# A two-block transformer on one core: expert outputs scaled as they leave PSUM and scattered by a one-hot matrix in two float32r parts

## The chip, the core and the metric

The kernel runs on one core of a Trainium2 chip. The core has a matrix engine (TensorE, "PE" in the profile; its weight loads appear as "PEld"), a vector engine (VectorE, "DVE"), a scalar engine (ScalarE, "ACT"), GpSimd ("POOL") and SyncE ("SP"), which here issues the weight DMAs. They share an on-chip memory, SBUF; PE writes its products to PSUM, and the other engines read them there. An f32 product takes PE several passes; a product of two "float32r" operands takes one, and a sum of a high and a low float32r part keeps nearly the precision of f32. The metric is the device time of one execution in microseconds (us).

## The reference

Two blocks follow each other on 256 tokens of width 1024. The first is an mLSTM mixer and a mixture of experts (MoE), the second a mixer of two kinds of attention and a feed-forward net. The change is in the experts. Each of 32 experts serves the tokens that have it among their four best, and its output is added to the token, times a gate:

```python
gate = xb @ w_gate[e] + b_gate[e]
up = xb @ w_up[e] + b_up[e]
gate = jnp.minimum(gate, SWIGLU_LIMIT)
up = jnp.clip(up, -SWIGLU_LIMIT, SWIGLU_LIMIT)
glu = gate * jax.nn.sigmoid(SWIGLU_ALPHA * gate)
return (glu * (up + 1.0)) @ w_down[e] + b_down[e]
...
y_buf = y_buf * gate_buf[:, None].astype(y_buf.dtype)
out = jax.ops.segment_sum(y_buf, tok_buf, num_segments=T + 1)[:T]
```

The weights of the experts are 32 x 12 MB of f32, and every one is read from HBM once.

## The kernel before

The first mixer and the router run until about 124 us, the experts from there to 1060 us, the second block to the end at 1650 us.

**Weights.** All weights of the program come through one ring of slots of 1 MB, in the order of their use (class `Ring`). SP's queue issues a slot's DMA as soon as the slot that it reuses is free (`refill`, called behind the products that used it). An expert has twelve such loads: four for `w_gate`, four for `w_up`, four for `w_down`.

**Tokens.** An expert works on at most CAP = 64 tokens at once. Two experts form a pair. `group(g)` makes the one-hot matrix `oh` of a pair (which token stands at which of the 128 places), gathers the tokens by products with it into `xg`, 128 columns at a time, multiplies the one-hot matrix by the gates (`og`, L1031) and transposes that with four PE transposes (L1040) into `sc`. A small scheduler hands out the steps of the next pair's `group` between the products of the current experts: `start` adds a generator, and `tick`, called after each slot of an expert's `up`, runs its next steps. `later`, which the kernel has for other stages, adds a function in the same way.

**An expert.** `up(e)` takes eight slots: sixteen products into `ps_g`, sixteen into `ps_u` (one PSUM buffer each, pool `psg`). `down(e-1)` begins: four transposes of the hidden vector into `ps_t`, and DVE's copy `ht`. `hidden(e)` calls `swiglu`, five operations on DVE and ACT, which read `ps_g` and `ps_u` and keep their temporary, `sg`, in SBUF. Then the four slots of `down(e-1)` follow, sixteen products into `ps_y`, and ACT copies those to `y`. After the second expert of a pair `down` also scatters: four f32 products of `sc` with `y` into `ps_x` (128 x 512 each), and four additions on DVE into the activations `x` (L1110).

```python
for e in range(n):
    ...
    for _ in up(e):
        ...
    if e:
        d = down(e - 1)
        next(d)
    hidden(e)
    if e:
        for _ in d:
            pass
```

Expert 0 has no `down` before it: expert 1's `up` follows expert 0's directly on PE.

**The biases of `w_down`.** `b_down()` computes gates times biases for all experts at once: two transposes of the gates (L996), and four f32 products added to `x` (L1004). Its 128 KB are loaded ahead of the experts, and the scheduler hands its steps out during experts 0 and 1.

**The end of the experts.** After the last scatter PE runs filler products of `ones` (`warm`, 14 of them, two passes each), then comes `overflow()`. That is code for experts with over 64 tokens; a branch on the largest count (L1159) jumps over it, as it does for these inputs. Behind the branch's target PE runs 12 more fillers, into `ps_b`, and then the twelve transposes of `fv` (L1309) with which the second block begins. The lines L106 and L109 are the helpers `act` and `mm`, through which most ACT operations and products go.

Of the kernel before, what the change touches and what calls it, by code (L numbers as in the profile page):

```python
# [92 lines left out]
class Kernel:  # L93
# [77 lines left out]
    def consts(self):  # L171
# [7 lines left out]
                                fill=1.0, base=0, channel_multiplier=1)  # L179
        self.nhalf = c.tile([128, 1], F32, name="nhalf")  # L180
# [745 lines left out]
    def top_gates(self, ps):  # L926
# [13 lines left out]
        for tb in range(2):  # L940
            v.tensor_scalar(out=gate[:, tb, :], in0=gate[:, tb, :], scalar1=sm[:, tb:tb + 1], scalar2=None,
                            op0=OP.mult)
        self.first_slot = p.tile([128, 2], F32, name="first_slot")
# [34 lines left out]
    def experts(self):  # L978
        nc, tc, a, x = self.nc, self.tc, self.a, self.x
        v = nc.vector  # L980
        with ExitStack() as ctx:
# [5 lines left out]
            pst = self.pool("mot", bufs=1, space=PSUM, ctx=ctx, reuse_waits="tile")  # L987

            bd = q.tile([E, D], F32, tag="y", name="bd", bufs=1)
            nc.scalar.dma_start(out=bd, in_=a["b_down"][0])  # L990
            gt = q.tile([E, T], F32, tag="ht", name="gt", bufs=1)

            def b_down():
# [4 lines left out]
                yield 2  # L998
                for tb in range(2):
                    for dh in range(2):  # L1000
# [4 lines left out]
                        yield  # L1005

            GR = 2
            xg, sc = {}, {}

            def group(g):  # L1010
# [9 lines left out]
                s = sc[g] = q.tile([128, GR // 2, 2, T], F32, tag="sc", name="sc")  # L1020
# [8 lines left out]
                og = q.tile([128, 2, GR // 2, 3, CAP], F32, tag="og", name="og", bufs=1)  # L1029
                for tb in range(2):  # L1030
                    v.tensor_tensor(out=og[:, tb, :, 0:2, :], in0=oh[:, tb].rearrange("p (a b) s -> p a b s", b=2),  # L1031
                                    in1=self.gate[:, tb, e0:e0 + GR].rearrange("p (a b) -> p a b", b=2)[
                                        :, :, :, None].to_broadcast([128, GR // 2, 2, CAP]), op=OP.mult)
                    nc.gpsimd.tensor_copy(og[:, tb, :, 2, :], og[:, tb, :, 0, :])
                yield 2
                for pr in range(GR // 2):
                    ps = psx.tile([128, 2, T], F32, tag="x", name="ps_x")
                    for i in range(2):
                        for tb in range(2):
                            nc.tensor.transpose(ps[:, i, tb * 128:(tb + 1) * 128],  # L1040
# [34 lines left out]
            def down(e):  # L1075
# [9 lines left out]
                if not odd:  # L1085
                    ys[e // 2] = q.tile([128, 2, 512], F32, tag="y", name="y", bufs=1)
# [1019 lines left out]
```

## Time and profile before

| | |
|---|---|
| median of 3 runs | 1653.11 us (1653.06 to 1653.57) |
| the profiled execution | 1652.3 us |
| its span, from first to last instruction | 1650.6 us |
| its mean granted TensorE clock | 0.994 |
| PE busy, share of the span | 95% |
| DVE, ACT, POOL busy | 42%, 32%, 3% |
| HBM traffic | 505.74 MB read, 307 GB/s over the span |

The shares are means over stages with different limits: the experts move over 400 GB/s, the second block under 210. Windows and timelines of a stage tell more than the totals. In a timeline, a row has its start, its length, the engine, the line, the operation, its output and inputs, and in brackets the idle time ahead of it and what ended that. The granted clock is a share of full speed: 1.00 is 2.4 GHz, 0.50 is 1.2 GHz.

### The profile page before, as it was taken

How to read it: one execution, taken by the hardware profiler on the slowest of the kernel's cores; microseconds unless marked ns; L12 is line 12 of the kernel's file. 1: busy time of each engine (PE TensorE's matmuls, PEld its weight loads, DVE VectorE, ACT ScalarE, POOL GpSimd, SP SyncE). 2: the span in 40 equal slices, each digit the busy share in tenths (PEclk: the TensorE clock that was granted, in tenths of full speed). 3: DMA queues.
4: the chain of work that ended last, by engine and by line, in shares of the span. 5: the costliest groups of instructions: out<-in, count | busy, mean ns of one | idle time of the engine just before them, and what ended most of it. 6: DMA issues, size and time to landing. Idle time of an engine off the chain costs nothing. (4 is left out here: it accounts for less than half of the span.)

```text
span 1650.6 us, 22396 instructions
## 1 busy us (share of the span) xinstructions
PE 1567.6 (95%) x8810; PEld 950.9 (58%) x8811; DVE 695.4 (42%) x1437; ACT 524.9 (32%) x1151; POOL 54.8 (3%) x124
## 2 busy tenths in 40 slices
PE   8999999999999999999999998799999999999997
PEld 8783333333333333333323322489888999989996
DVE  6862212212121212122121121388875376777775
ACT  4562111111111111111111110256663356565554
POOL 0100000000000000000000010000111010000000
PEclk9999999999999999999999999999999999999999
DMA  8878999999999999999999999644343333556551
GB/s 285 305 307 310 408 418 421 421 422 421 420 422 420 421 421 422 421 420 421 421 421 421 421 421 421 271 131 155 124 153 103 103 120 137 179 166 202 182 187 69
DMA packets 119235, 508.31 MB, mean 308 GB/s; under 512 B 10364, under 2 KB 33717, under 8 KB 70101
## 3 DMA queue, kind: packets, MB, share of 16 engines
q1 hardware_dynamic: 117284, 506.01, 77.8%
q8 instruction: 71, 1.16, 0.3%
q10 hardware_dynamic: 1840, 0.82, 0.2%
q14 instruction: 40, 0.32, 0.1%
HBM read 505.74 MB, written 1.05 MB: 307 GB/s over the span
## 5 line engine op out<-in xcount | busy, mean ns | idle before, releaser
L349 DVE TENSOR_TENSOR lo<-w,hi 128x512 fp32r<-128x512 f32 (+2 forms) x380 | 257.3, 691 | 56.9 <-PE ps_d L109 30.6
L1081 DVE COPY ht<-ps_t 128x512 f32<-128x512 f32 x32 | 22.1, 692 | 596.5 <-PE ps_t L1079 596.5
L109 PE MATMUL ps_y<-w,ht 128*64 128x512 f32 x1024 | 230.1, 597 | 29.8 <-DVE ht L1081 25.1
L106 ACT ACTIVATE hi<-w 128x512 fp32r<-128x512 f32 (+2 forms) x380 | 232.1, 628 | 74.8 <-PE ps_d L109 67.2
L109 PE MATMUL ps_g<-w,xg 128*64 128x512 f32 x1024 | 238.3, 600 | 6.1 <-DMA w<-in_w_gate_dram 4.9
L109 PE MATMUL ps_u<-w,xg 128*64 128x512 f32 x1024 | 238.0, 600 | 2.9 <-DMA w<-in_w_up_dram 2.8
L109 PEld LDWEIGHTS ps_y<-w,ht 128*64 128x64 f32 x1024 | 69.2, 136 | 170.0 <-issue 113.6
L106 ACT ACTIVATE xg<-ps_x,n2p 128x128 f32<-128x128 f32 x128 | 47.0, 368 | 334.3 <-PE ps_x L109 334.0
L109 PEld LDWEIGHTS ps_g<-w,xg 128*64 128x64 f32 x1024 | 67.1, 136 | 135.2 <-issue 101.0
L109 PEld LDWEIGHTS ps_u<-w,xg 128*64 128x64 f32 x1024 | 66.1, 136 | 116.6 <-issue 96.3
L109 PEld LDWEIGHTS ps_x<-oh,xn 128*128 128x128 f32 x512 | 68.7, 190 | 78.2 <-issue 64.7
L106 ACT ACTIVATE y<-ps_y 64x512 f32<-64x512 f32 x64 | 37.9, 592 | 186.7 <-PE ps_y L109 186.1
L109 PE MATMUL ps_x<-oh,xn 128*128 128x128 f32 x512 | 86.9, 294 | 0.8 <-DVE oh L1016 0.8
L106 ACT ACTIVATE sg<-gg 128x512 f32<-128x512 f32 x32 | 20.1, 629 | 200.4 <-DVE gg L1262 200.3
L1110 DVE TENSOR_TENSOR x<-x,ps_x 128x512 f32<-128x512 f32 x64 | 43.9, 686 | 91.9 <-PE ps_x L109 91.9
L109 PE MATMUL ps_d<-hnh,hi 128*128 128x256 f32 x448 | 77.7, 295 | 0.8 <-ACT hi L106 0.5
L109 PE MATMUL ps_d<-hnh,lo 128*128 128x256 f32 x448 | 71.5, 281 | 3.2 <-DVE lo L349 3.1
L109 PE MATMUL ps_d<-hnl,hi 128*128 128x256 f32 x448 | 71.1, 281 | 0.0
L109 PE MATMUL ps_x<-y,sc 128*128 128x512 f32 x128 | 59.2, 605 | 11.1 <-ACT y L106 11.1
L109 PEld LDWEIGHTS ps_d<-hnh,hi 128*128 128x128 f32 x448 | 61.5, 189 | 3.5 <-ACT hi L106 0.6
L109 PEld LDWEIGHTS ps_d<-hnh,lo 128*128 128x128 f32 x448 | 60.7, 188 | 4.0 <-DVE lo L349 3.8
L109 PEld LDWEIGHTS ps_d<-hnl,hi 128*128 128x128 f32 x448 | 60.8, 188 | 0.2
(435 smaller groups left out, 2079.3 us busy)
## 6 DMA issues: line engine op xcount, KB each, us to landing
w<-in_w_down_dram SPq DMA_DIRECT2D x137, 1024.0 KB
w<-in_w_gate_dram SPq DMA_DIRECT2D x128, 1024.0 KB
w<-in_w_up_dram SPq DMA_DIRECT2D x128, 1024.0 KB
w<-in_w_in_dram SPq DMA_DIRECT2D x40, 1024.0 KB
w<-in_w_up_dram SPq DMA_DIRECT2D x44, 512.0 KB
w<-in_w_out_dram SPq DMA_DIRECT2D x8, 1024.0 KB
w<-in_w_branch_gdn_dram SPq DMA_DIRECT2D x4, 1024.0 KB
w<-in_w_branch_fox_dram SPq DMA_DIRECT2D x4, 1024.0 KB
```

The costliest lines, as they stand in the source:

```text
L106: self.nc.scalar.activation(out=out, in_=in_, func=func, **kw)
L109: self.nc.tensor.matmul(out, lhsT=lhsT, rhs=rhs, start=start, stop=stop, **kw)
L349: nc.vector.tensor_tensor(out=lo[:, :n], in0=src, in1=hi[:, :n].bitcast(F32), op=OP.subtract)
L1081: v.tensor_copy(ht, ps)
L1110: v.tensor_tensor(out=o, in0=o, in1=ps, op=OP.add)
```

## The change

The gate no longer goes into the matrix that scatters. `og` is now the one-hot matrix itself in bf16. A new generator `back(g)`, run in the second expert of a pair, transposes it by four bf16 products with an identity (`ident16`, one per program) into `sc`, and gets the gate of each place by four more small products, with the gates cut into three bf16 parts (`gate3`), which DVE sums to `gc`. As `ps_y` leaves PSUM, ACT multiplies it by the gate into `y`, a float32r tile, and DVE computes what that rounding lost into a second one, `yl`. The scatter is then two float32r products, with `y` and `yl`, where it was one f32 product. For all pairs but the third and the last it is handed to `later`, which spreads it over the next expert's `up`. `b_down` is loaded at the end of the loop's turn for expert 6 (counted from 0) and summed in the turn of expert 7, the eighth, between its `up` and the products of `down(6)`. Because the tiles' memory is needed elsewhere, `swiglu` gets its temporary from its caller: in the experts this is `ps_g` itself.

```diff
-
-            bd = q.tile([E, D], F32, tag="y", name="bd", bufs=1)
-            nc.scalar.dma_start(out=bd, in_=a["b_down"][0])
-            gt = q.tile([E, T], F32, tag="ht", name="gt", bufs=1)
-
             def b_down():
+
+                bd = q.tile([E, D], F32, tag="y", name="bd", bufs=1)
+                nc.scalar.dma_start(out=bd, in_=a["b_down"][0])
+                yield
+                gt = q.tile([E, T], F32, tag="ht", name="gt", bufs=1)
                 ps = psx.tile([128, 512], F32, tag="x", name="ps_x")
                 for tb in range(2):
                     nc.tensor.transpose(ps[0:E, tb * 128:(tb + 1) * 128], self.gate[:, tb, :], self.ident)
                 v.tensor_copy(gt, ps[0:E, 0:T])
-                yield 2
+                yield
                 for tb in range(2):
                     for dh in range(2):
                         ps = psx.tile([128, 512], F32, tag="x", name="ps_x")
                         self.mm(ps, gt[:, tb * 128:(tb + 1) * 128], bd[:, dh * 512:(dh + 1) * 512])
                         o = x[:, tb, dh * 512:(dh + 1) * 512]
                         v.tensor_tensor(out=o, in0=o, in1=ps, op=OP.add)
-                        yield
 
             GR = 2
-            xg, sc = {}, {}
+            xg, og, sc, gc = {}, {}, {}, {}
...
-                s = sc[g] = q.tile([128, GR // 2, 2, T], F32, tag="sc", name="sc")
...
-                og = q.tile([128, 2, GR // 2, 3, CAP], F32, tag="og", name="og", bufs=1)
-                for tb in range(2):
-                    v.tensor_tensor(out=og[:, tb, :, 0:2, :], in0=oh[:, tb].rearrange("p (a b) s -> p a b s", b=2),
-                                    in1=self.gate[:, tb, e0:e0 + GR].rearrange("p (a b) -> p a b", b=2)[
-                                        :, :, :, None].to_broadcast([128, GR // 2, 2, CAP]), op=OP.mult)
-                    nc.gpsimd.tensor_copy(og[:, tb, :, 2, :], og[:, tb, :, 0, :])
-                yield 2
-                for pr in range(GR // 2):
-                    ps = psx.tile([128, 2, T], F32, tag="x", name="ps_x")
-                    for i in range(2):
-                        for tb in range(2):
-                            nc.tensor.transpose(ps[:, i, tb * 128:(tb + 1) * 128],
-                                                og[:, tb, pr].rearrange("p e s -> p (e s)")[:, i * CAP:i * CAP + 128],
-                                                self.ident)
-                    self.act(s[:, pr], ps)
-                    yield
+                o = og[g] = q.tile([128, 2, 3, CAP], BF16, tag="og", name="og", bufs=1)
+                v.tensor_copy(o[:, :, 0:2, :], oh)
+                v.tensor_copy(o[:, :, 2, :], oh[:, :, 0, :])
+
+            def back(g):
+
+                o = og.pop(g).rearrange("p b e s -> p b (e s)")
+                s = sc[g] = q.tile([128, 2, T], F32R, tag="sc", name="sc", bufs=1)
+                c = gc[g] = q.tile([128, 2, 2], F32, tag="gc", name="gc", bufs=1)
+                ps = psx.tile([128, 2, T], F32, tag="x", name="ps_x")
+                for i in range(2):
+                    for tb in range(2):
+                        self.mm(ps[:, i, tb * 128:(tb + 1) * 128], o[:, tb, i * CAP:i * CAP + 128], self.ident16)
+                self.act(s, ps)
+                yield
+                ps = psx.tile([128, 512], F32, tag="x", name="ps_x")
+                for i in range(2):
+                    for tb in range(2):
+                        self.mm(ps[:, i * 6:i * 6 + 6], o[:, tb, i * CAP:i * CAP + 128],
+                                self.gate3[:, tb, g * GR:g * GR + GR, :].rearrange("p e k -> p (e k)"),
+                                start=tb == 0, stop=tb == 1)
+                v.tensor_reduce(out=c, in_=ps[:, 0:12].rearrange("p (i e k) -> p i e k", i=2, e=2),
+                                axis=mybir.AxisListType.X, op=OP.add)
...
             def hidden(e):
                 gg = q.tile([128, 512], F32, tag="gg", name="gg", bufs=1)
-                self.swiglu(gg, *hs[e])
+                self.swiglu(gg, *hs[e], hs[e][0])
                 hs[e] = gg
...
                 odd = e % 2
                 if not odd:
-                    ys[e // 2] = q.tile([128, 2, 512], F32, tag="y", name="y", bufs=1)
-                y = ys[e // 2]
+                    ys[e // 2] = [q.tile([128, 2, 512], F32R, tag=t, name=t, bufs=1) for t in ("y", "yl")]
+                y, yl = ys[e // 2]
+                c = gc[e // 2]
...
                 for h in range(2):
                     r = (h ^ odd) * 64
-                    self.act(y[r:r + 64, h, :], pa[r:r + 64, :])
+                    self.act(y[r:r + 64, h, :], pa[r:r + 64, :], scale=c[r:r + 64, h, odd:odd + 1])
+                for h in range(2):
+                    r = (h ^ odd) * 64
+                    v.scalar_tensor_tensor(out=yl[r:r + 64, h, :], in0=pa[r:r + 64, :], scalar=c[r:r + 64, h, odd:odd + 1],
+                                           in1=y[r:r + 64, h, :].bitcast(F32), op0=OP.mult, op1=OP.subtract)
                 if odd:
-                    yield
-                    g, i = divmod(e - 1, GR)
-                    for h in range(2):
-                        for tb in range(2):
-                            ps = psx.tile([128, 512], F32, tag="x", name="ps_x")
-                            self.mm(ps, sc[g][:, i // 2, h, tb * 128:(tb + 1) * 128], y[:, h, :])
-                            o = x[:, tb, h * 512:(h + 1) * 512]
-                            v.tensor_tensor(out=o, in0=o, in1=ps, op=OP.add)
-                            if e == n - 1:
-                                rest.append(self.mid_sums(xsq, gf2, h, tb))
-                                for gen in rest[-2:]:
-                                    next(gen, None)
+                    if e in (n - 1, B_DOWN - 1):
+                        for _ in scatter(e):
+                            yield
+                    else:
+                        self.later(1, scatter, e)
+
+            def scatter(e):
+                y, s = ys.pop(e // 2), sc[e // 2]
+                for h in range(2):
+                    for tb in range(2):
+                        ps = psx.tile([128, 512], F32, tag="x", name="ps_x")
+                        for i in range(2):
+                            self.mm(ps, s[:, h, tb * 128:(tb + 1) * 128], y[i][:, h, :], start=i == 0, stop=i == 1)
+                        o = x[:, tb, h * 512:(h + 1) * 512]
+                        v.tensor_tensor(out=o, in0=o, in1=ps, op=OP.add)
+                        if e == n - 1:
+                            rest.append(self.mid_sums(xsq, gf2, h, tb))
+                            for gen in rest[-2:]:
+                                next(gen, None)
                         yield
...
                 if e % GR == 0 and e + GR < n:
                     self.start(group(e // GR + 1))
-                for _ in up(e):
+                way = iter(back(e // GR)) if e % GR else None
+                bd = b_down() if e == B_DOWN else bd
+                for k, _ in enumerate(up(e)):
                     if e == 0 and first:
                         for _ in range(2):
                             if next(first, 0) == 0:
                                 first = None
-                                self.start(b_down())
                                 break
                     else:
                         self.tick(2 if e < 2 * GR else 1)
+
+                    if way and k > 4:
+                        next(way, None)
+                if bd and e > B_DOWN:
+                    for _ in bd:
+                        pass
+                    bd = None
                 if e:
                     d = down(e - 1)
                     next(d)
@@ -1139,6 +1174,8 @@
                 if e:
                     for _ in d:
                         pass
+                if e == B_DOWN:
+                    next(bd)
             self.drain()
...
-    def swiglu(self, gg, pg, pu, paired=False):
+    def swiglu(self, gg, pg, pu, t, paired=False):

 
         v = self.nc.vector
-        t = self.mow.tile([128, 512], F32, tag="sg", name="sg", bufs=1)
...
+B_DOWN = 6
```

PE at the end of expert 0 and the start of expert 1, before (`ps_g` and `ps_u` are the products of `up`, `oh` those of the gather, `lg` the gates, `bd` the biases):

```order
L1040 MATMUL ps_x<-ident,og 128x128 x4
L109 MATMUL ps_u<-w,xg 64x512 x8
L996 MATMUL ps_x<-ident,lg 32x128 x2
L109 MATMUL ps_u<-w,xg 64x512 x4
L109 MATMUL ps_x<-oh,xn_1557 128x128 x2
L109 MATMUL ps_u<-w,xg 64x512 x4
L109 MATMUL ps_u<-bias,pick 128x512
L109 MATMUL ps_x<-bd,gt 128x512
L109 MATMUL ps_x<-oh,xn_1557 128x128 x2
L109 MATMUL ps_g<-w,xg 64x512 x4
```

The same place with the change:

```order
L109 MATMUL ps_u<-w,xg 64x512 x8
L109 MATMUL ps_x<-oh,xn_1559 128x128 x2
L109 MATMUL ps_u<-w,xg 64x512 x4
L109 MATMUL ps_x<-oh,xn_1559 128x128 x2
L109 MATMUL ps_u<-w,xg 64x512 x4
L109 MATMUL ps_u<-bias,pick 128x512
L109 MATMUL ps_x<-oh,xn_1559 128x128 x2
L109 MATMUL ps_g<-w,xg 64x512 x4
```

The transposes of `og` and of the gates and the bias product are gone from here, and one more step of the gather stands ahead of expert 1.

DVE from one expert's `ht` over `swiglu` on, before:

```order
L1081 COPY ht<-ps_t 128x512
L1262 TENSOR_SCALAR gg<-ps_g 128x2x128x2
L1264 TENSOR_TENSOR gg<-gg,sg 128x512
L1268 TENSOR_SCALAR sg<-ps_u 128x2x128x2
L1269 SCALAR_TENSOR_TENSOR gg<-sg,gg 128x512
```

And with the change:

```order
L1095 COPY ht<-ps_t 128x512
L1298 TENSOR_SCALAR gg<-ps_g 128x2x128x2
L1300 TENSOR_TENSOR gg<-gg,ps_g 128x512
L1304 TENSOR_SCALAR ps_g<-ps_u 128x2x128x2
L1305 SCALAR_TENSOR_TENSOR gg<-ps_g,gg 128x512
L1119 SCALAR_TENSOR_TENSOR yl<-ps_y,gc,y 64x512 x2
```

The last reader of `ps_g` is now the fourth of the DVE operations, not the first, and two operations for `yl` follow.

PE at the end of the experts, before (the last `down`, the scatter, the fillers, the branch of L1159):

```order
L109 MATMUL ps_y<-w,ht 64x512 x16
L109 MATMUL ps_x<-y,sc 128x512 x4
L109 MATMUL ps_x<-ones 128x128 x14
L1158 TENSOR_LOAD cmax
L1159 COMPARE_AND_BRANCH
```

With the change:

```order
L109 MATMUL ps_y<-w,ht 64x512 x16
L109 MATMUL ps_x<-y,sc 128x512
L109 MATMUL ps_x<-yl,sc 128x512
L109 MATMUL ps_x<-y,sc 128x512
L109 MATMUL ps_x<-yl,sc 128x512
L109 MATMUL ps_x<-y,sc 128x512
L109 MATMUL ps_x<-yl,sc 128x512
L109 MATMUL ps_x<-y,sc 128x512
L109 MATMUL ps_x<-yl,sc 128x512
L109 MATMUL ps_x<-ones 128x128 x14
L1195 TENSOR_LOAD cmax
L1196 COMPARE_AND_BRANCH
```

The scatter's four products are now eight; the fillers and the branch follow as before.

## Rows read from the trace of the kernel before

**Rows 1.** Windows: stretch, us, PE, PEld, DVE, ACT, POOL busy, clock, DMA share, GB/s.
```profile
949.00:990.00 41.00, 37.25 (x160) 12.16 (x158) 9.24 (x14) 4.47 (x9) 5.09 (x4) 1.00 1.01 422
1072.00:1114.00 42.00, 41.52 (x304) 36.97 (x303) 34.45 (x81) 25.10 (x52) 4.00 (x8) 1.00 0.41 128
```

**Rows 2.** The page: GB/s in 40 equal slices of the span.
```profile
GB/s 285 305 307 310 408 418 421 421 422 421 420 422 420 421 421 422 421 420 421 421 421 421 421 421 421 271 131 155 124 153 103 103 120 137 179 166 202 182 187 69
```

**Rows 3.** Waits of PE, 900 to 1000 us: us in all, how many, the longest.
```profile
PE ps_g L109 <- DMA w<-in_w_gate_dram: 3.3, 6, 0.6
```

**Rows 4.** Timeline of PE: the transposes of og, and a scatter.
```profile
561.38 0.60 PE L1040 MATMUL ps_x<-ident,og 128*128 128x128 f32 x4
...
606.32 3.70 PE L109 MATMUL ps_x<-y,sc 128*128 128x512 f32 x8 [0.69 <-ACT y L106]
```

**Rows 5.** Timeline of PE: float32r products of the first mixer.
```profile
100.33 0.40 PE L109 MATMUL ps_o<-hi,yph 128*128 128x512 f32 x1
100.56 0.40 PE L109 MATMUL ps_o<-lo,yph 128*128 128x512 f32 x1
```

**Rows 6.** Timeline: one down on PE, the last operation of swiglu on DVE.
```profile
570.65 7.09 PE L109 MATMUL ps_y<-w,ht 128*64 128x512 f32 x32 [0.78 <-DVE ht L1081]
...
574.15 0.69 DVE L1269 SCALAR_TENSOR_TENSOR gg<-sg,gg 128x512 f32<-128x512 f32 x1
```

**Rows 7.** Windows of 5 us at the start of the stream.
```profile
125.00:130.00 5.00, 4.99 (x31) 2.54 (x31) 1.69 (x12) 2.09 (x7) 0.41 (x2) 1.00 0.36 115
...
180.00:185.00 5.00, 5.00 (x26) 1.91 (x24) 0.00 (x0) 2.28 (x5) 0.00 (x0) 1.00 0.99 403
```

**Rows 8.** Timeline: the end of expert 0 and the start of expert 1.
```profile
146.24 1.12 PE L109 MATMUL ps_x<-bd,gt 32*128 32x512 f32 x2
...
148.00 1.03 DVE L1262 TENSOR_SCALAR gg<-ps_g 128x512 f32<-128x512 f32 x1
...
148.43 1.28 ACT L106 ACT_TABLE_LOAD   x1
...
149.09 1.94 PE L109 MATMUL ps_g<-w,xg 128*64 128x512 f32 x8 [1.09 <-DVE gg L1262]
...
149.72 0.63 ACT L106 ACTIVATE sg<-gg 128x512 f32<-128x512 f32 x1
```

**Rows 9.** Timeline: the last scatter on ACT and DVE.
```profile
1053.32 1.21 ACT L106 ACTIVATE y<-ps_y 64x512 f32<-64x512 f32 x2 [8.13 <-PE ps_y L109]
...
1055.13 0.69 DVE L1110 TENSOR_TENSOR x<-x,ps_x 128x512 f32<-128x512 f32 x1 [9.92 <-PE ps_x L109]
```

**Rows 10.** Timeline: the handover from the experts to the second block.
```profile
1057.50 3.29 PE L109 MATMUL ps_x<-ones 128*128 128x128 f32 x28
...
1061.24 1.24 PE L109 MATMUL ps_b<-ones 128*128 128x128 f32 x9 [0.45 <-PEq L1159]
...
1064.49 0.34 DVE L1302 TENSOR_SCALAR fv<-x,nr 128x256 f32<-128x256 f32 x1
...
1066.41 3.57 PE L109 MATMUL ps_b<-ones 128*128 128x128 f32 x15 [3.93 <-issue]
...
1069.77 2.44 PE L1309 MATMUL ps_t<-ident,fv 128*128 128x128 f32 x12
```

**Rows 11.** DMA queues, 1062.5 to 1066.4 us: packets, MB, share of 16 engines.
```profile
q8 instruction: 1, 0.02, 1.9%
```

**Rows 12.** Windows: the rest of the fillers and the transposes.
```profile
1066.40:1072.00 5.60, 5.59 (x28) 5.60 (x28) 0.26 (x1) 1.14 (x3) 0.00 (x0) 0.52 0.02 5
```

**Rows 13.** The page: busy us and instructions by engine; the queue of instructions.
```profile
PE 1567.6 (95%) x8810; PEld 950.9 (58%) x8811; DVE 695.4 (42%) x1437; ACT 524.9 (32%) x1151; POOL 54.8 (3%) x124
...
q8 instruction: 71, 1.16, 0.3%
```

**Rows 14.** Timeline of PE: the first twelve transposes of the program.
```profile
9.85 1.59 PE L1309 MATMUL ps_t<-ident,qk 128*128 128x128 f32 x12 [0.65 <-DVE qk L1298]
```

**Rows 15.** A window of 5 us late in the experts.
```profile
1010.00:1015.00 5.00, 3.53 (x17) 0.91 (x14) 0.00 (x0) 0.86 (x2) 0.00 (x0) 1.00 1.01 419
```

More of the change, by code (lines that the diff above doesn't have):

```diff
@@ L179, in consts @@
                                 fill=1.0, base=0, channel_multiplier=1)
+        self.ident16 = c.tile([128, 128], BF16, name="ident16")
+        nc.vector.tensor_copy(self.ident16, self.ident)
         self.nhalf = c.tile([128, 1], F32, name="nhalf")
@@ L942, in top_gates @@
                             op0=OP.mult)
+        self.gate3 = p.tile([128, 2, E, 3], BF16, name="gate3")
+        rest = p.tile([128, 2, E], F32, name="grest", tag="gate")
+        v.tensor_copy(self.gate3[:, :, :, 0], gate)
+        v.tensor_tensor(out=rest, in0=gate, in1=self.gate3[:, :, :, 0], op=OP.subtract)
+        v.tensor_copy(self.gate3[:, :, :, 1], rest)
+        v.tensor_tensor(out=self.gate3[:, :, :, 2], in0=rest, in1=self.gate3[:, :, :, 1], op=OP.subtract)
         self.first_slot = p.tile([128, 2], F32, name="first_slot")
@@ L1064, in up @@
                         if k0 == KD - 2:
-                            self.mm(ps, pick.rearrange("p h s -> p (h s)"), self.bias[:, m, :], start=False, stop=True,
-                                    skip_group_check=True)
+                            self.mm(ps, pick.rearrange("p h s -> p (h s)"), self.bias[:, m, :],
+                                    start=False, stop=True, skip_group_check=True)
                         yield
@@ L1134, in experts @@
                         self.tick(2 if e < 2 * GR else 1)
+                    if way and k > 4:
[3 more added lines that the diff above has]
+                        pass
+                    bd = None
                 if e:
@@ L1181, in overflow_block @@
         oh = q.tile([128, 2, CAP], F32, tag="oh", name="ooh", bufs=1)
-        og = q.tile([128, 2, 2, CAP], F32, tag="og", name="oog", bufs=1)
+        place = q.tile([128, D], F32, tag="yl", name="oplace", bufs=1)
+        og = place[:, 512:768].rearrange("p (b i s) -> p b i s", b=2, i=2)
         for tb in range(2):
@@ L1187, in overflow_block @@
                                 op0=OP.mult)
-        xt = q.tile([128, KD, CAP], F32, tag="sc", name="oxt")
+        xt = q.tile([128, KD, CAP], F32, tag="sc", name="oxt", bufs=1)
         ps = psx.tile([128, KD, CAP], F32, tag="x", name="ps_x")
@@ L1207, in overflow_block @@
         gu = []
-        for name, bn, tag, place in (("w_gate", "b_gate", "g", "gg"), ("w_up", "b_up", "u", "sc")):
+        for name, bn, tag in (("w_gate", "b_gate", "g"), ("w_up", "b_up", "u")):
             b = q.tile([128, 512], F32, tag="ht", name="ob", bufs=1)
@@ L1218, in overflow_block @@
                             start=k == 0, stop=k == KD - 1)
-            t = q.tile([128, 512], F32, tag=place, name="og_u", bufs=1 if place == "gg" else None)
+            t = place[:, 0:512] if tag == "u" else q.tile([128, 512], F32, tag="gg", name="og_u", bufs=1)
             v.tensor_tensor(out=self.pairs(t), in0=self.plain(ps), in1=self.plain(b), op=OP.add)
@@ L1222, in overflow_block @@
         gg = gu[0]
-        self.swiglu(gg, *gu, paired=True)
+        self.swiglu(gg, *gu, psg.tile([128, 512], F32, tag="g", name="ps_g"), paired=True)
         ps = pst.tile([128, 512], F32, tag="t", name="ps_t")
```

## The prediction, as put on record

> **What bounds the kernel now.** First the windows over the span and the page's row of GB/s, to see which engine or queue is full in which stage [rows 1, 2]. From about 185 us to 1047 us the DMA engines are full (1.01 of their time) and move 421 GB/s in every slice: the weights of the 32 experts. PE looks nearly as busy there, but it keeps time with the weights. Then PE's waits in the last third of that stage [rows 3]: six waits for `w_gate` in 100 us, at most 0.6 us each. PE has caught up with the stream and idles a little before the weights. An expert's twelve slots are 12.6 MB, 29.9 us at 421 GB/s. So until 1047 us the stream is the bound, and work taken from PE there only lengthens its waits. From 1072 us on PE is the bound (41.52 of 42 us, DMA 0.41): whatever moves the start of that stage moves the end. The time can therefore change in three places only: the start of the stream (125 to 185 us), the bytes in it, and the handover between 1053 and 1072 us.
>
> **The change, part by part.** *PE in the experts.* A pair loses eight passes of the f32 scatter (3.70 us), PE's wait of 0.69 us for `y` ahead of them, and four `og` transposes (0.60 us) [rows 4]. It gains eight float32r products, which start 0.23 us apart [rows 5], 1.85 us, and eight small bf16 products. For these no row stands; between the 0.15 us of a transpose [rows 4] and nothing I take 0.1 each. That is 3.70 + 0.69 + 0.60 - 1.85 - 0.80 = 2.3 us less per pair, 37 us over 16 pairs. I cost it at nothing: the stream covers it. If that cover were gone it would be worth the whole 37 us. DVE gains two `yl` operations per expert, 0.69 us each like the 128x512 operation of `swiglu` [rows 6], and is idle most of the stage (fourth column) [rows 1].
>
> *The start of the stream.* Between 125 and 185 us the stream is not full: over twelve windows of 5 us the DMA shares fall short of 1 by 6.8 us in all; the emptiest and the last stand in the table [rows 7]. The queue waits there for PE to free slots, so 6.8 us is the most that an earlier PE could win. Moving `b_down` to expert 8 takes four products from this place, 1.12 us each [rows 8], three of them inside expert 1, and two transposes. The `og` transposes go from expert 0 into expert 1 in their new form. Against that stands a new wait. `swiglu` now keeps its sigmoid, and then its clipped up half, in `ps_g`, of which there is one buffer. So expert 1's first product into `ps_g` waits for the last operation of expert 0's `swiglu`, where it now waits for the first alone (it ends at 149.03). For later experts this costs nothing: a `down` of 7.09 us lies between, and `swiglu` ends 4.2 us into it [rows 6]. Ahead of expert 1 no `down` lies. Following the timeline [rows 8]: the sigmoid needs its table load (1.28) and 0.63, as now, so with the first transposes gone it ends near 149.1; then 0.69, 1.03 (the row of L1262) and 0.69 with their gaps. Expert 1 starts at 151.7 instead of 149.09, 2.6 us late. Inside its `up` it then has three products of 1.12 less, two gathers (1.3, moved ahead) less and the small products 0.9 more: 3.8 us less, so PE reaches `down(0)` 1.2 us earlier. Not all of that arrives: the last short place of the stream comes after it, at the first scatter, which is spread over the next `up` and gives only tenths. I take a third, **-0.4 us**; the ends are -4.6 (no new wait) and +2.6 (the wait alone).
>
> *The bytes in the stream.* `b_down`'s 128 KB were loaded ahead of 125 us; now they travel in the full stream: 0.13 MB / 421 GB/s = **+0.3 us**. The 5 us of PE that expert 8 then spends on them lie in slack, since PE has saved over 1 us in each expert until there.
>
> *The last scatter.* After the last `ps_y` product two ACT copies follow, then four products and DVE's adds [rows 9]. Now DVE has two `yl` operations (1.4 us) ahead of the first add: it starts 2.06 us after the last product instead of 1.83, and later adds no longer wait for PE. **+0.1 us**, ends -0.3 and +0.7 (one operation).
>
> *The handover, through the position of a branch.* Here lies the largest term, and no line of the diff says so. After the last scatter PE runs 28 filler passes, branches over the overflow code (L1159), and runs 24 more before the transposes that open the next stage [rows 10]. It gets through nine of the 24, then stands for 3.93 us though it waits for nothing that the profile shows ("issue"). In that gap one packet of the instruction queue lands [rows 11], and the clock falls to the lower of its levels, 1.2 GHz [rows 12]: the other fifteen passes take 3.57 us, 0.238 each against 0.117 in the 28 before, and the transposes start at 1069.77. Their input `fv` was ready at 1064.8. The page counts 71 such packets, 16 KB each, for the program's 18,184 PE instructions, 17,621 of them loads and products [rows 13]: 256 to a packet. The order of PE's instructions shows where such a block ended: 21 past the branch's target (three waits, nine loads, nine products), just where PE stood. The next block had been asked for only when PE arrived in that one.
>
> The change puts 139 instructions more on PE ahead of the branch (8 for each of 16 pairs, and 11 waits); between branch and target there are some 338, as before. Blocks end at the same counts, so the target now stands 256 - (139 - 21) = 138 ahead of a block's end. The 24 filler passes (48 instructions) and 12 transposes (24) fit in, with some 30 products of the next stage: time to fetch what follows. The price is that the target's own block is asked for late: its predecessor begins 36 instructions ahead of the branch, 18 filler passes, 2.1 us of PE. From asking to use the rows give 3.9 us (from the last pass before the gap, 1062.48) to 5.2 us (from the first after the branch, 1061.24). So the target's block is there between 1062.6 and 1063.9, a shorter stall of 1.4 to 2.7 us after the branch; I take 1062.9, nearer the early end, since the sequencer runs ahead of PE. Then 24 x 0.117 = 2.8 us, transposes at 1065.7, 4.1 us earlier, and at full clock they take 1.59 us [rows 14], not the 2.44 of before [rows 10]. **-4.9 us**. The ends: no stall at all, transposes when the 24 passes end at 1064.0 (or with `fv` at 1064.8), -6.6; a stall of 2.7 us with the clock lost, 1063.9 + 24 x 0.238 = 1069.6, -0.2.
>
> The Trainium skill, "Runtime: NRT & Kernel Launch", "Instruction fetch mechanics", says that code comes in blocks of 256 instructions, that a window of two blocks is filled in sequence, and that a taken branch to a target outside it makes the engine wait for the fetch. The trace agrees in block and in stall [rows 10, 11], though there the target itself was still in the window. Whether a block on its way counts as inside, the page does not say; by its strict reading the third rival below would be the forecast.
>
> **The sum.** Against the profiled run's own 1652.3 us (span 1650.6 and 1.7 around it): -0.4 + 0.3 + 0.1 - 4.9 = -4.9, 1647.4. The median of the runs shown, 1653.1, stands 0.8 above that run, so **1648.2 us**.
>
> **Rivals.**
> 1. *The fetch stall only moves*: its block lands at the late end and the clock falls, or another place stalls. What is left is the stream, 0.0 in all: 1653.1, no change. For it: in the gap of the trace the clock fell [rows 10, 12], and mine is a gap too.
> 2. *PE is a bound after all*, and its 37 us count: 1611. Against it: 421 GB/s flat, and the waits for `w`.
> 3. *The block on its way is dropped and asked for again at the target*: PE resumes at 1066.4 as now, but with all 24 passes at the lower clock, 5.7 us: transposes at 1072.1, +2.3, hence **1655.4, slower than before**. It decides in the one gap behind L1159.
> 4. *The clock falls in the experts*: PE now idles over 2 us in each 29.9, and in a stretch granted 1.2 GHz its 27 us an expert double, past the stream: over 20 us for each expert so hit, 1673 for one and more for several. Against it: from 1010 to 1015 us PE had only 3.53 of 5 us, and clock 1.00 [rows 15]. The Trainium skill, "TensorE: Matmul & The Clock Gate", Part 1, says that idling takes the clock down, and shows a kernel that waits for each slice of weights and falls every time; this trace has such waits and no fall [rows 15].
>
> **How the numbers follow.** Forecast 58 in 100; rival 1 26; rival 2 2; rival 3 9; rival 4 3; unnamed mishaps in the new order 2. A measurement of this kernel tells 0.2% (3.3 us) from no change: 1649.8 and 1656.4 are the borders. The forecast's own range is 1645.6 to 1649.8. To hold 8 in 10 the range must reach over rival 1, whose stream term may shift it by 0.8: 1645.6 to 1653.9. Faster: the forecast and rival 2, 60. Same: rivals 1 and 3, 35. Slower by over 0.2%: rival 4 and the mishaps, 5.
>
> **What would show it.** Right: DMA still at 421 GB/s to about 1047 us; PE's waits for `w` longer, and earlier in the stage; a gap behind the branch ahead of the first filler pass, under 3 us; clock 1.00 there; transposes near 1066. Wrong: a gap of 4 us after some passes or ahead of them; clock near 0.5 from 1065 to 1070; expert 1 starting after 153 us; a stretch of the experts under 415 GB/s.

## The result, and the profile after

The changed kernel takes 1662.43 us (median of 4 runs, 1661.63 to 1663.45), before 1653.09: a ratio of 1.0057, interval 1.0039 to 1.0074. Forecast were 1648.2 and 1645.6 to 1653.9. It is **slower by 9.3 us**, and the forecast had the wrong sign. The profiled execution took 1661.9 us, its span is 1660.2, 9.6 above that of before.

First the windows of the expert stage, in the columns of [rows 1]. Before:

```profile
125.00:200.00 75.00, 73.10 (x345) 29.10 (x344) 13.54 (x32) 14.13 (x34) 0.82 (x4) 1.00 0.91 355
300.00:345.00 45.00, 42.74 (x196) 16.55 (x196) 8.94 (x13) 5.41 (x13) 0.41 (x2) 1.00 1.01 422
345.00:1045.00 700.00, 660.32 (x2972) 241.08 (x2968) 143.59 (x216) 89.91 (x198) 9.18 (x24) 1.00 1.01 421
```

After:

```profile
125.00:200.00 75.00, 69.25 (x329) 27.50 (x327) 12.42 (x34) 14.06 (x34) 0.00 (x0) 0.95 0.88 338
...
300.00:345.00 45.00, 41.88 (x189) 15.70 (x186) 8.70 (x16) 5.07 (x11) 0.00 (x0) 0.96 0.73 300
345.00:1045.00 700.00, 657.17 (x3010) 235.07 (x3010) 172.00 (x279) 93.32 (x197) 4.68 (x2) 1.00 1.01 425
```

The last column gives three differences. The start of the stream lost 75 x (355 - 338) / 425 = 3.0 us. A hole that did not exist before, 300 to 345 us, cost 45 x (422 - 300) / 425 = 12.9. And where the stream is full it is faster, 425 instead of 421 GB/s, which gave back some 7 us. The three make about 9; the stream's last bytes land 8 us later. The first of them is uncertain, since single traces differ there: the kernel before, run again, moved 345 GB/s from 125 to 200 us, by which the start lost 1.2 and not 3.0. Beside the two losses the clock is no longer 1.00.

The timeline around the start of expert 1 answers to [rows 8]:

```profile
150.74 0.69 DVE L1305 SCALAR_TENSOR_TENSOR gg<-ps_g,gg 128x512 f32<-128x512 f32 x1
151.54 3.68 PE L109 MATMUL ps_g<-w,xg 128*64 128x512 f32 x8 [4.67 <-issue]
155.15 1.23 PE L109 MATMUL ps_x<-oh,xn 128*128 128x128 f32 x4
```

PE waits for the last operation of `swiglu`, which reads `ps_g` and ends at 151.43, and starts at 151.54 (forecast: 151.7). The profile names no releaser here ("issue"); the experiment with expert 0's temporary shows that it is this one. The gap of 4.67 us is followed by passes of twice the length: eight take 3.68 us, where eight took 1.94. The clock in this stretch is 0.50, the lower level of 1.2 GHz:

```profile
150.00:155.00 5.00, 3.46 (x8) 0.86 (x8) 1.39 (x2) 0.00 (x0) 0.00 (x0) 0.50 0.40 169
```

For the hole at 300 us, the waits of SP's queue from 295 to 330 us (us in all, how many, the longest), and its timeline:

```profile
SPq L53 <- DMA bd<-in_b_down_dram: 27.3, 1, 27.3
```

```profile
297.98 30.97 SPq L53 DMA_DIRECT2D w<-in_w_down_dram  x4
329.04 2.15 SPq L53 DMA_DIRECT2D w<-in_w_gate_dram  x4
```

SP issues four `w_down` loads from 297.98 on, and needs 31 us for the four, since one of them waits 27.3 us for the load of `b_down` to land. That load stands on ACT's queue and leaves it only at 325.30, when the scatter of the third pair has freed its place (tag `y`):

```profile
325.30 0.32 ACTq L1000 DMA_DIRECT2D bd<-in_b_down_dram  x1
```

The last expert shows a third loss. DVE and PE in the timeline, after:

```profile
1051.35 0.66 PE L1093 MATMUL ps_t<-ident,gg 128*128 128x128 f32 x4
...
1052.93 1.52 DVE L1119 SCALAR_TENSOR_TENSOR yl<-ps_y,gc,y 64x512 fp32r<-64x512 f32 x2 [5.91 <-ACT y L106]
...
1054.48 0.69 DVE L1095 COPY ht<-ps_t 128x512 f32<-128x512 f32 x1
...
1055.23 10.08 PE L109 MATMUL ps_y<-w,ht 128*64 128x512 f32 x32 [3.22 <-DVE ht L1095]
```

The `yl` operations of expert 31 (of 32) stand ahead of expert 32's `ht` on DVE. PE waits 3.22 us, the clock falls again, and the last `down` takes 10.08 us, where one takes 7.09 [rows 6]. Its end moves from 1053.27 to 1065.31, by 12.0: about 4 more than the stream.

Last the handover, which answers to [rows 10]:

```profile
1070.33 3.86 PE L109 MATMUL ps_x<-ones 128*128 128x128 f32 x28
...
1075.72 2.92 PE L109 MATMUL ps_b<-ones 128*128 128x128 f32 x24 [1.53 <-PEq L1196]
...
1078.47 1.47 PE L1345 MATMUL ps_t<-ident,fv 128*128 128x128 f32 x12
```

In this execution the forecast's picture holds: the gap stands behind the branch, is 1.53 us long, all 24 passes follow at full speed, and the transposes take 1.47 us. From the end of the last `down` to the transposes it is 13.16 us, before 16.50: 3.3 gained. The scatter, at the lower clock, takes 0.8 of that back; from the first filler to the transposes it is 8.14 us against 12.27, 4.1 less. The sum over the places is 12.0 - 3.3 = 8.7; the last 0.9 of the 9.6 comes later in the second block. The transposes themselves are 1.0 shorter, so 1.9 us are lost behind them. The runs below do not repeat this short gap.

### The profile page after: what moved, and what is told of

Its sections match the earlier page's. It is cut to its first block, busy times and chain, and to the rows that moved or that the text cites. A ratio compares the mean times of both kernels' runs of the same rounds, so it can differ in the third digit from the quotient of the medians.

```text
span 1660.2 us, 22546 instructions
## 1 busy us (share of the span) xinstructions
PE 1569.0 (95%) x8874; PEld 945.9 (57%) x8875; DVE 732.7 (44%) x1522; ACT 529.4 (32%) x1151; POOL 47.7 (3%) x92
## 5 line engine op out<-in xcount | busy, mean ns | idle before, releaser
L109 PE MATMUL ps_y<-w,ht 128*64 128x512 f32 x1024 | 237.2, 610 | 33.0 <-DVE ht L1095 27.5
L109 PE MATMUL ps_g<-w,xg 128*64 128x512 f32 x1024 | 247.8, 608 | 18.6 <-DMA w<-in_w_gate_dram 13.5
L109 PE MATMUL ps_u<-w,xg 128*64 128x512 f32 x1024 | 244.5, 603 | 4.1 <-DMA w<-in_w_up_dram 4.1
L1119 DVE SCALAR_TENSOR_TENSOR yl<-ps_y,gc,y 64x512 fp32r<-64x512 f32 x64 | 48.0, 750 | 175.4 <-ACT y L106 174.6
L106 ACT ACTIVATE y<-ps_y,gc 64x512 fp32r<-64x512 f32 x64 | 43.7, 682 | 199.7 <-PE ps_y L109 199.1
L1037 DVE CAST og<-oh 128x256 bf16<-128x256 f32 x16 | 4.7, 292 | 171.6 <-PE ps_x L109 171.6
L106 ACT ACTIVATE ps_g<-gg 128x512 f32<-128x512 f32 x32 | 19.2, 601 | 147.3 <-DVE gg L1298 147.3
L106 ACT ACTIVATE sc<-ps_x 128x512 fp32r<-128x512 f32 x16 | 9.6, 597 | 172.4 <-PE ps_x L109 172.4
```

The lines of the kernel that those rows point to most:

```text
L106: self.nc.scalar.activation(out=out, in_=in_, func=func, **kw)
L109: self.nc.tensor.matmul(out, lhsT=lhsT, rhs=rhs, start=start, stop=stop, **kw)
L1037: v.tensor_copy(o[:, :, 0:2, :], oh)
L1119: v.scalar_tensor_tensor(out=yl[r:r + 64, h, :], in0=pa[r:r + 64, :], scalar=c[r:r + 64, h, odd:odd + 1], in1=y[r:r + 64, h, :].bitcast(F3 ...
```

## The experiments

Three theories of a loss each had an edit that takes it away and leaves the rest. The times of before beside them were 1653.2, 1653.0 and 1652.3 us.

**The kernel before again**, for the rate of the stream.

> The kernel before, unchanged, beside the others on one chip. In the changed kernel's trace the expert stream runs at 425 GB/s, in the first trace of before at 421. If the rate belongs to the change (fewer passes of PE, less work on GpSimd), this run shows 421 again and 1653. If it belongs to the chip or the run, it shows 425 somewhere in the stage, and the end of the experts comes up to 8 us earlier.

1654.48 us in the one run, and 421 GB/s from 400 to 1000 us. So the rate belongs to the change, not to the chip or the run; more of it below.

**The load of `b_down` on another queue.**

```diff
-                nc.scalar.dma_start(out=bd, in_=a["b_down"][0])
+                nc.gpsimd.dma_start(out=bd, in_=a["b_down"][0])
```

> The changed kernel with the load of b_down issued by GpSimd's queue instead of ACT's. Theory: the weight queue stood from 301 to 328 us because its next load reuses the completion semaphore that the b_down load had taken, and that load waits for the pair buffer y. On another queue it has another semaphore: the stretch 300 to 345 us is full (share 1.0, it was short by 12.9 us), and the time falls by about 12.9 to 1649.5 (1648 to 1651). Rival: the wait belongs to the load itself or to the pair buffer, whichever queue issues it: the stretch stays empty, 1662.4.

1650.63 us (ratio to before 0.9979, 0.9962 to 0.9996): 11.8 less than the changed kernel. The hole is gone:

```profile
300.00:345.00 45.00, 41.88 (x190) 15.79 (x187) 9.87 (x17) 4.96 (x11) 0.75 (x1) 1.00 1.01 419
```

The load still waits for the same place and moves the same bytes; it no longer holds SP. How it held SP stands in the changed program's order, here SP's rows 115 to 117 and 123, and ACT's row 182, with what each waits for:

```
115 L53 DMA w<-in_w_gate_dram 128x2048 [waits DMAHW1_49,PE_49]
116 L53 DMA w<-in_w_gate_dram 128x2048 [waits DMAHW3_49,PE_49]
117 L53 DMA w<-in_w_up_dram 128x2048 [waits DMAHW4_49,PE_49]
...
123 L53 DMA w<-in_w_down_dram 128x2048 [waits DMAHW2_49,PE_49]

182 L1000 DMA bd<-in_b_down_dram 32x1024 [waits DMAHW2_49,PE_49,Activation_49]
```

The loads of SP and ACT take eight completion semaphores (DMAHW0 to 7) in turn. `bd` took number 2 between rows 115 and 116. Row 123 is the next user and must see it landed. SP runs ahead of the consumers by many slots, so it came to row 123 at 300.8 us, 25 us before ACT could issue `bd`.

**Expert 0's temporary out of `ps_g`.**

```diff
-                self.swiglu(gg, *hs[e], hs[e][0])
+                t = hs[e][0] if e else q.tile([128, 2, 512], F32, tag="yl", name="sg", bufs=1)[:, 0, :]
+                self.swiglu(gg, *hs[e], t)
```

> The changed kernel, but expert 0 alone keeps its swiglu temporary in SBUF (in the place of yl, which nothing uses yet). Theory: expert 1's first product starts at 149.1 instead of 151.5, the gap of PE is 2 us or less, the clock stays 1.00 from 150 to 160 us, and the stream is short by some 3 us less until 200 us: 1659.3 (1658.3 to 1660.5). Rival: PE is ahead of the stream there anyway, and the gap only takes the place of later waits: 1662.4.

1655.27 us (1.0012, 1.0002 to 1.0022): 7.2 less, over twice what the theory gave. PE and the windows:

```profile
147.06 1.94 PE L109 MATMUL ps_g<-w,xg 128*64 128x512 f32 x8
```

```profile
125.00:200.00 75.00, 73.14 (x362) 29.54 (x363) 16.52 (x39) 15.31 (x37) 0.00 (x0) 1.00 0.94 383
```

Expert 1 starts at 147.06, without any gap. Counted from there the wait had cost 151.54 - 147.06 = 4.5 us, and the clock 3.68 - 1.94, 1.23 - 0.71 and 0.2 in the passes behind it, 2.5: together 6.9. The stream moves 383 GB/s in its start, 28 above before: 75 x 28 / 425 = 4.9 us better than before (6.7 against the 345 GB/s of before run again). The prediction's end for "no new wait" was -4.6.

**The last `ht` ahead of `yl`.**

```diff
+                for fn in low:
+                    fn()
+                low.clear()
...
-                for h in range(2):
+                def lows():
...
+                if e == n - 2:
+                    low.append(lows)
+                else:
+                    lows()
```

> The changed kernel, but the two yl operations of the last expert but one come behind DVE's copy ht of the last expert. Theory: the last down starts 1.5 us or more earlier, PE's gap ahead of it is 0.8 instead of 3.2 us, the clock stays 1.00, and its last product ends with the last weights, about 0.5 us behind 1061.4 instead of at 1065.3: 1659.0 (1658 to 1660.5). Rival: the last down waits for its weights, so that an earlier start is worth nothing: 1662.4.

1658.52 us (1.0034, 1.0021 to 1.0047): 3.9 less, as the theory said. PE, timeline:

```profile
1052.49 3.65 PE L109 MATMUL ps_y<-w,ht 128*64 128x512 f32 x16 [0.78 <-DVE ht L1095]
...
1056.65 3.65 PE L109 MATMUL ps_y<-w,ht 128*64 128x512 f32 x16 [0.50 <-DMA w<-in_w_down_dram]
```

**All three edits.**

> The changed kernel with the three edits together (b_down on GpSimd's queue, expert 0's temporary in SBUF, the last ht ahead of yl). Theory: they remove three separate gaps, so their gains add: 11.8 + 7.2 + 3.9 = 22.9 us less than 1662.4, 1639.5 (1637.5 to 1641.5). Rival: two of them hide in each other (an earlier start of the stream only makes the weight queue wait longer elsewhere): 1643 or more.

1639.19 us (0.9902, 0.9865 to 0.994). The gains add within 0.3 us, so the three are separate, and the change without them is 14 us faster than before. The rival falls. The 14 us are nearly accounted for: 75 x (385 - 355) / 425 = 5.3 at the start of the stream, some 7 by its rate, and 1.4 from the last `down` to the transposes (15.10 us, before 16.50).

At the branch this run is not like the trace of the changed kernel. The fillers ahead of it and behind it:

```profile
1044.68 3.39 PE L109 MATMUL ps_x<-ones 128*128 128x128 f32 x28
...
1051.31 4.38 PE L109 MATMUL ps_b<-ones 128*128 128x128 f32 x24 [3.24 <-PEq L1208]
```

The gap is 3.24 us and the clock falls in it. So it is in the three runs with one edit each (gaps of 2.80 to 3.47 us, then 4.54 us for the 24 passes), although the branch stands at the same place. From the first filler to the transposes the four take 10.6 to 11.3 us, 1.0 to 1.7 less than before, where the changed kernel's trace had 4.1 less.

**The branch alone, 137 instructions later**, in the kernel before:

```diff
+                    if 26 <= e < 31 and k < 7:
+                        self.warm(psx.tile([128, 512], F32, tag="x", name="ps_x"), 1)
```

> The kernel before with 35 filler products of 128 x 128 in experts 26 to 30, where PE waits for weights: 137 instructions more ahead of the branch, so that the target stands 140 instead of 21 instructions ahead of a block's end, and nothing else changes. Theory of the prediction: a stall of 1.4 to 2.7 us right behind the branch, clock 1.00, 1648.2. What the runs so far suggest: the stall behind the branch is 2.8 to 3.5 us and the clock falls in it, which leaves 1 us: 1652 (1651 to 1653). Rival (the position of the branch does nothing): 1653.1, with a gap of 3.9 us after nine passes.

1651.56 us (0.9985, 0.9969 to 1.0001): 1.4 less, unclear against no change. PE's timeline behind the branch:

```profile
1058.43 3.29 PE L109 MATMUL ps_x<-ones 128*128 128x128 f32 x28
1064.93 2.92 PE L109 MATMUL ps_b<-ones 128*128 128x128 f32 x24 [3.21 <-PEq L1161]
1067.69 1.47 PE L1311 MATMUL ps_t<-ident,fv 128*128 128x128 f32 x12
1068.92 0.36 PE L109 MATMUL ps_s<-hnh,hi 128*8 128x256 f32 x1
```

The stall stands where the forecast put it, before the first pass, and the clock holds, but it is 3.21 us, not 1.4 to 2.7. The target's block was asked for 33 instructions ahead of the branch, some 16 passes of 0.117 before the fillers' end at 1061.72, at 1059.8; PE goes on at 1064.93. That is 5.1 us, at the late end of the prediction's bracket of 3.9 to 5.2. Counted in the same way, from 18 passes before the fillers' end, it was 3.6 us in the changed kernel's trace and 4.9 to 5.6 in the four runs above with one or all of the edits. The block's packet stands in the trace. In the instruction queue, from 1061.9 to 1063.0 us:

```profile
q8 instruction: 1, 0.02, 5.7%
```

It ends at 1062.95, and PE goes on 2.0 us later; behind the branch these are 1.9 to 2.1 us in all six runs with a gap there so far.

**The branch alone, 190 instructions later** (as above, from expert 24 on).

> As the run before, but 49 filler products (experts 24 to 30), about 190 instructions: the target's block is entered 50 instructions earlier before the branch than in the run before, and 85 to 87 instructions are left in it behind the target. Theory (a block is asked for when the one ahead of it is entered, and takes some 4 us): both fetches are covered, no gap over 1 us, clock 1.00, the transposes start at about 1064.9 in the times of before instead of 1069.8: 1647.5 (1646 to 1649). Rival (the branch always drops what is on its way): a gap of 3 us or more stays, 1652 or more.

1648.54 us (0.9966, 0.9951 to 0.9981), 4.4 less than before:

```profile
1057.45 3.29 PE L109 MATMUL ps_x<-ones 128*128 128x128 f32 x28
1061.18 2.92 PE L109 MATMUL ps_b<-ones 128*128 128x128 f32 x24 [0.45 <-PEq L1161]
1063.94 1.50 PE L1311 MATMUL ps_t<-ident,fv 128*128 128x128 f32 x12
```

With the block entered 50 instructions sooner nothing is left but the branch itself, 0.45 us: the block's packet had landed at 1052.45, 8 us ahead of the branch. Only filler products were added, where PE waits for weights. So the position of a branch in the code is worth 4.4 us here, and a block that has landed is not dropped by a taken branch.

The prediction's third rival is about a block still on its way, which this run does not have. The run with the last `ht` first has it: its packet travels from 1067.81 to 1068.75, PE's fillers end at 1067.94, and PE goes on at 1070.74 without a second packet in between. Every run of this study has 71 such packets, as before [rows 13], so no block was fetched twice: the third rival falls.

**The slots at their old addresses.** The tile `ident16` goes behind the first twelve weight slots:

```diff
-        self.ident16 = c.tile([128, 128], BF16, name="ident16")
+        self.ident16 = p.tile([128, 128], BF16, name="ident16")
```

> The three edits, and the tile ident16 (256 bytes per partition) moved behind the first twelve weight slots, so that these twelve stand at the SBUF addresses of before (256 bytes lower) and the other seven where the changed kernel has them. Theory: the rate of 425 instead of 421 GB/s comes from where the slots lie: the rate falls back to 421 or to between 421 and 425, and the time is 3 to 7 us above that of the three edits. Rival (the rate comes from less work of PE or GpSimd): 425 and the same time.

1639.93 us (0.9905, 0.9867 to 0.9943) and 425 GB/s: moving the first twelve slots by 256 bytes does nothing. In either place they begin 160 bytes behind a multiple of 256.

**The last seven slots 128 bytes higher**:

```diff
+        pad = p.tile([128, 32], F32, name="pad")
+        v.memset(pad, 0.0)
```

> The three edits, and 128 unused bytes ahead of the last seven weight slots, which so begin at 128 instead of 0 behind a multiple of 512 bytes (before: 384). Theory: the 425 GB/s come from these seven lying on a multiple of 512: the rate falls to 421 to 423, the time rises by 3 to 7 us. Rival (nothing in the addresses): 425 and 1639.

1646.55 us, 7.4 more than without the pad; it is one run, so this time has no interval. The windows from 400 to 1000 us, first with the three edits alone:

```profile
400.00:1000.00 600.00, 569.72 (x2644) 206.44 (x2642) 147.27 (x240) 82.12 (x175) 4.68 (x2) 1.00 1.01 425
```

With the 128 bytes:

```profile
400.00:1000.00 600.00, 566.30 (x2620) 204.64 (x2616) 143.65 (x236) 82.07 (x174) 4.68 (x2) 1.00 1.01 421
```

The rate falls back to 421 by an unused pad alone. The pad moves all tiles behind it by 128 bytes, not the seven slots only; the last section has what the packets say to that.

**Before, without copies on GpSimd**:

```diff
-                    nc.gpsimd.tensor_copy(og[:, tb, :, 2, :], og[:, tb, :, 0, :])
+                    v.tensor_copy(og[:, tb, :, 2, :], og[:, tb, :, 0, :])
```

> The kernel before, with the two copies of og per pair on DVE instead of GpSimd, as the changed kernel has none on GpSimd. Theory: work of GpSimd beside the stream costs the 1%: the rate rises to 425, and the time falls by up to 8 us to 1645. Rival: 421 and 1653.

1653.11 us in the one run, 421 GB/s: the copies on GpSimd have no part in it.

**The three edits and the branch moved** by 15 filler products in experts 27 to 29:

> The three edits, and 15 filler products in experts 27 to 29, which put the branch's target 81 instead of 136 instructions ahead of a block's end and its block 55 instructions earlier before the branch, as in the run with 49 fillers. Theory: the stall behind the branch (3.24 us) goes and the fillers run at full clock, the transposes start 6.3 us behind the last scatter instead of 10.7: 4.4 less than 1639.2 at that place, of which about 0.9 is lost right behind it as in the run with 49 fillers: 1635.5 (1634.5 to 1637). Rival: what starts earlier waits for the weights of the second block, 1638 or more.

1637.16 us (0.9907, 0.9891 to 0.9924), the lowest median of the study, 15 below the runs of before beside it and 25 below the changed kernel; its interval overlaps that of the three edits alone. The stall is gone, but against 1639.2 only 2.0 us are won and not 3.7 (1.4, if each is set against the runs of before beside it):

```profile
1047.10 4.38 PE L109 MATMUL ps_x<-ones 128*128 128x128 f32 x28
1051.92 2.92 PE L109 MATMUL ps_b<-ones 128*128 128x128 f32 x24 [0.45 <-PEq L1210]
1054.68 1.25 PE L1359 MATMUL ps_t<-ident,fv 128*128 128x128 f32 x10
1056.30 0.38 PE L1359 MATMUL ps_t<-ident,fv 128*128 128x128 f32 x2 [0.37 <-issue]
```

The first fillers take 4.38 us instead of 3.39, for here the clock falls in the last scatter, where PE waits 0.78 us for `y` and 1.00 for `yl` (with the three edits alone the same waits stand there, and the clock falls only in the gap behind the branch); and the next block's end now stands within the transposes, ten of them in, for 0.37 us.

## Why the prediction was wrong, point by point

*PE in the experts, 37 us hidden*: right. The stream was the bound in every run, PE's waits for weights from 400 to 1000 us grew from 8.9 to 17.9 us in all, and the second rival (1611) was far off.

*The start of the stream, -0.4*: wrong, +3.0 in the trace (+1.2 against before run again), and here the first step failed. The start of expert 1 was forecast to 0.2 us (151.54), but priced as 2.6 us against the old start. Without the wait PE would have started at 147.06, and behind a gap of 4.67 us it ran at the lower clock. The wait cost 7 us, not 2.6. Of the two ends, "no new wait" was about right in size (-4.9 to -6.7 measured, -4.6 given).

*The fourth rival, the clock falling in the experts*, had 3 in 100. Its place was sought in the steady waits for weights, where the clock stayed at 1.00 from 400 to 1000 us in the trace of after too, and not in the new wait that the prediction itself had worked out. The Trainium skill's rule on idling ("TensorE: Matmul & The Clock Gate", Part 1) was weighed against the wrong gaps: the waits of that page's example are several times longer than the 0.6 us of [rows 3], so these could not speak against the rule; the gap of 4.67 us, with 0.50 behind it, agrees with it. The clock fell at a third place as well, in the turn of expert 7, to which the change moved the products with the biases:

```profile
343.81 3.67 PE L109 MATMUL ps_x<-bd,gt 32*128 32x512 f32 x8 [0.55 <-issue]
...
348.88 9.98 PE L109 MATMUL ps_y<-w,ht 128*64 128x512 f32 x32 [0.79 <-DVE ht L1095]
```

A `down` takes 9.98 us there instead of 7.09; in the seven other runs of the changed kernel it takes 8.4 to 10.0. The stream moved 419 GB/s or more in the windows of the fall, so no loss of the stream shows, and it is far from the 20 us of that rival.

*The bytes in the stream, +0.3*: wrong by a term of 12.9, which the prediction put at nothing. It counted the bytes of `b_down` and PE's work, but not who waits for the load to land. The experiment with the other queue (11.8 less) shows the price; that a shared completion semaphore carries the wait is read from the order of the program and SP's wait row, and agrees with that run.

*The last scatter, +0.1*: right for the scatter itself (4.26 us from the last `down` to the first filler with the three edits, 4.23 before), but some 4 us were missed just ahead of it. The two `yl` operations were placed ahead of the first addition of the last expert, but those of the expert before it were not followed: they stand ahead of the last `ht` (3.9 less with `ht` first).

*The handover, -4.9*: too large, and only partly right in mechanism. The stall did move behind the branch, with no pass ahead of it. That the gap is short and the clock holds came true in the changed kernel's own trace: 4.1 us less up to the transposes and 1.0 less in them, of which 1.9 are lost again behind them. This was luck. In the four runs with one or all of the edits and the branch at the same place the gap was 2.80 to 3.47 us, the clock fell, and 1.0 to 1.7 us were left, which is nearer to the first rival. In the kernel before, with the branch alone moved so, the gap was 3.21 us, the clock held, and the run won 1.4 with an interval that reaches no change. Two parts of the term were mis-sized: the time from asking for a block to PE going on, 4.9 to 5.6 us in these runs where the forecast took 4.2, and the passage of the gain to the end, which was taken as whole. The Trainium skill ("Runtime: NRT & Kernel Launch", "Instruction fetch mechanics") left open whether a block on its way counts; by the packets of these runs it does.

*Not in the prediction at all*: the stream's rate, 425 for 421 GB/s, some 7 us in the change's favour.

## What to carry to other kernels

When a load moves to a later place in the program, ask what its completion holds up, not only what bytes it adds: a load that waits for its buffer can park a queue of others that share its semaphores. Price a new wait of several microseconds on PE with the passes behind it at the lower clock, and count it from where PE could have started. When operations are added at the end of a step, follow them into the next step on the same engine, the last one above all.

## What the runs showed of the hardware

The stream's rate hangs on the place of some of the weight slots in SBUF. By their addresses in the programs, the last seven of the nineteen slots begin 384 bytes behind a multiple of 512 in the kernel before, on a multiple of 512 in the changed one, and 128 behind with the pad. Kernels with them on the multiple ran at 425 GB/s (after, and every run of it with one or all of the three edits but no pad), the others at 421 (before in both runs, its three variants, and the pad). A multiple of 256 would fit these three places as well.

The packets in the traces show that the slots carry it, and not some other tile that the pad moved. From 400 to 1000 us a packet of 8 KB took 311 ns in the mean in each of the kernels at 425 GB/s, and 314 in those at 421. In the first kind the short packets, of 309 ns, come in stretches that return every 19 loads, the length of the ring; in the second nothing returns so. But some twelve loads in nineteen are short, not seven. Why, and where the one per cent comes from, is open; a layout with all nineteen on such a multiple was not tried.

The clock did not follow the length of a gap alone. A gap of 3.21 us left it at 1.00 in one run (24 passes in 2.92 us), and gaps of 2.8 to 3.5 us at the same branch were followed by a fall in the runs with the changed scatter (4.38 to 4.54 us for the 24). The scatter ahead of the gap does not decide it either: with the old one, in the run without copies on GpSimd, a gap of 3.19 us was followed by fifteen passes in 3.06 us, 0.20 each instead of 0.117. And the clock fell in the turn of expert 7, as shown above and in all eight traces of the changed kernel, with no gap over 0.8 us ahead, at or right behind eight passes that use 32 rows of PE (32 x 128); in the kernel before the same eight stand in pairs between products of the weights, and the clock stayed at 1.00. That these passes are the cause is likely and not shown.
